# The odd mixer's modulation loads behind four input loads, and the S5 input matrix with weights and moving operand exchanged

## The chip, the core and the metric

The kernel runs on one core of a Trainium2 chip. The metric is the device time of one execution in microseconds (us): before, the median of three runs is 1391.2 us, the runs lie between 1390.48 and 1392.53. The engines named below are TensorE (PE in the rows: matmuls and transposes), VectorE (DVE), ScalarE (ACT), GpSimd (POOL) and SyncE (SP), whose queue issues most of the DMA transfers.

## The reference: what is computed

One step of a two-layer hybrid recurrent decoder for a prompt of 512 tokens and 8 single-token samples, model width 1024. Each layer has a mixer and a SwiGLU FFN, both with shift, scale and gate rows ("modulation") from a conditioning vector, and a layer norm behind each. Layer 0 mixes with gated linear attention beside an RG-LRU, layer 1 with an S5 state space model beside HGRN2. Cut to what matters here:

```python
mod = jnp.einsum('bd,de->be', cond, w_ada[l]) + b_ada[l]
sh_m, sc_m, gt_m, sh_f, sc_f, gt_f = [m[:, None, :] for m in jnp.split(mod, 6, axis=-1)]
h = x * (1.0 + sc_m) + sh_m
...
z = jnp.einsum('bld,de->ble', h, w_in).astype(jnp.float32)
u, q, f, i, g = split_cols(z, ODD_SPLITS)
y, s_re_new, s_im_new = s5_ssm(u, s_re, s_im, lam_re, lam_im, log_dt, b_re, b_im, c_re, c_im, d_skip)
...
x = layer_norm(ALPHA * x + (1.0 + gt_m) * out, ln_g[l, 0], ln_b[l, 0])
h = x * (1.0 + sc_f) + sh_f
x = layer_norm(ALPHA * x + (1.0 + gt_f) * swiglu(h, ffn_w_in[l], ffn_w_out[l]), ln_g[l, 1], ln_b[l, 1])
```

`s5_ssm` is a complex-diagonal recurrence over 32 groups of 16 channels and 64 states. The kernel runs it by chunks of eight tokens, with matrices worked out from the S5 parameters alone: the matrix from one chunk's inputs to the state, from the state to its outputs, and from inputs to outputs within a chunk.

## The kernel before

**Columns and halves.** Activations lie with channels on the partitions and 520 columns: two halves of 260, each 256 prompt tokens and four samples. A weight matrix product is done in three passes on values that are split into a high and a low part (`mm3`, lines 237 to 241, and `mmh`, lines 816 to 818, which takes one half at a time): weights 128x128, 260 columns moving.

**The weight stream.** All large weights come in one order, the list `plan` (from line 266). Each entry is one load of up to 1 MB on SyncE's queue (line 176) into one of three raw buffers. An "in", "fin" or "fout" entry is then split by ScalarE (`whi`, line 199) and VectorE (`wlo`, line 110) into one of three slots. An "ada" entry is a piece of the modulation weights: its eight matmuls (line 323, 32 weight columns each, in four column strips of TensorE) run straight from the raw buffer, and four such entries make one chunk of 1024 modulation columns, which ScalarE copies (`adasb`), TensorE transposes twice (line 147) and VectorE adds to its bias (`mod`). `mix(main, ada, first, per)` spreads the ada entries among the main ones: `first` main entries come ahead, then ada entries, `per` at a time. Line 287 does that for the odd mixer's ten input loads (`OD_COLS`: first columns 0, 256, 1024, 1280, 512, ...) and eight ada entries (`OA`: the gate of the mixer and the shift of the FFN of layer 1).

**What sets the order.** The kernel is recorded once, and a scheduler then sets the order of the instructions on every engine from its own model of their times; so an edit in one place can move others on all engines.

**The S5 preparation.** `s5_prep` works out the S5 matrices during the first half of layer 0's FFN, between that FFN's matmuls. For each of four chunks of eight groups: VectorE makes `BA` (three operations of 128x1024, with the temporary `W`), TensorE transposes it eight times (for `BATd`), and then eight matmuls (line 1620) multiply `BA` as weights (128x128 per group) with `CS` as the moving operand (16 columns per group) into `pM`, from which ScalarE copies 128x128 into `Mall` (line 1622). VectorE goes on with `CA` and `W`. `BA`, `W`, `CA` and `sb` share four buffers. `Mall` is read behind all four chunks. In the same stretch VectorE serves the FFN: `sg` multiplies a finished accumulator by its gate and so frees it, `al` is the low part of the product that the FFN's output projection (`ah`, `al`) reads.

**The passage to the odd mixer.** Layer 0's FFN ends in a layer norm, done half by half. `odd_mixer` begins with `first_units`: five units of 128 output columns (four of u, one of f), half 0 first, while the layer norm of half 1 still runs. For u the accumulator is emptied by ScalarE (`ut`, line 1671) and VectorE (`u_s`, line 1673), and for each 128 channels `Ud` is written to DRAM (line 1675), then `Usd` (line 1695). Eight gathers (line 1697) and two more (lines 1698, 1699) read them back into `u8`, all on SyncE's queue, and `s5_in` (line 1716) multiplies u8 with `BATd`. Between these the remaining units of f, q, i and g run with `mm3`. The layer norm's matmuls are lines 699 to 702.

## Time and profile before

| what | value |
|---|---|
| median of three runs | 1391.2 us (1390.48 to 1392.53) |
| the profiled execution | 1391.37 us |
| its span | 1389.4 us |
| TensorE busy | 1333.4 us (96%) |
| VectorE busy | 764.9 us (55%) |
| ScalarE busy | 498.2 us (36%) |
| GpSimd busy | 191.8 us (14%) |

The rows are of one profiled execution; its span begins with the first and ends with the last instruction, and 2.0 us of its time lie around it. All starts are us from the span's start. The median is 0.17 us under the profiled execution.

### The profile page before, as it was taken

The page shows a single profiled execution, that of the slowest core. Times are in us where ns is not written, and L with a number is a line of the kernel's source. Part 1 is how long each engine was busy: PE and PEld are TensorE (multiplying, and loading weights), DVE is VectorE, ACT ScalarE, POOL GpSimd, SP SyncE. Part 2 cuts the span into 40 slices and gives each one's busy share as a digit, 9 for nine tenths or more (in the row PEclk, how much of TensorE's full clock was granted, in tenths as well). Part 3 has the DMA queues.
Part 4 walks back from the last instruction along what each step waited for, and adds up shares of the span by engine and source line. Part 5 has one row for each costly group of instructions (what it writes and reads, how often), then busy time and mean ns, then how long its engine had stood idle before and what let it go on. Part 6 is the DMA issues. An engine that isn't in the chain of part 4 may idle for free. (4 is left out here: it accounts for less than half of the span.)

```text
span 1389.4 us, 29467 instructions
## 1 busy us (share of the span) xinstructions
PE 1333.4 (96%) x12687; PEld 1267.0 (91%) x12687; DVE 764.9 (55%) x1726; ACT 498.2 (36%) x802; POOL 191.8 (14%) x215
## 2 busy tenths in 40 slices
PE   6998999989999999999998999999999999999996
PEld 4797988989998999999988999889899999999996
DVE  4677755687997233233592785566833233232365
ACT  3555536353232222222264123363533222222231
POOL 2200010340011200000170421013500000000013
PEclk9999999999999999999999999999999999999998
DMA  9643363413345842444458446432333323221211
GB/s 277 197 152 101 91 212 120 154 48 120 116 166 205 234 152 92 152 133 158 150 200 169 131 147 216 126 126 92 101 113 107 118 95 122 92 92 54 84 62 63
DMA packets 157628, 185.53 MB, mean 134 GB/s; under 512 B 18188, under 2 KB 137354, under 8 KB 157242
## 3 DMA queue, kind: packets, MB, share of 16 engines
q1 hardware_dynamic: 151514, 166.43, 38.7%
q0 software_dynamic: 5744, 17.08, 3.8%
q8 instruction: 100, 1.64, 0.5%
q14 instruction: 30, 0.25, 0.1%
q10 hardware_dynamic: 240, 0.13, 0.0%
HBM read 167.11 MB, written 15.36 MB: 131 GB/s over the span
## 5 line engine op out<-in xcount | busy, mean ns | idle before, releaser
L237 PE MATMUL acc<-hhi,whi 128*128 128x260 f32 x1936 | 398.8, 287 | 3.0 <-ACT whi L199 1.3
L199 ACT CAST whi<-raw 128x1024 fp32r<-128x1024 f32 (+2 forms) x198 | 187.7, 955 | 587.1 <-PE acc L239 428.1
L239 PE MATMUL acc<-hlo,whi 128*128 128x260 f32 x1936 | 396.2, 286 | 1.2 <-DVE hlo L110 1.2
L241 PE MATMUL acc<-hhi,wlo 128*128 128x260 f32 x1936 | 395.1, 285 | 0.0
L110 DVE TENSOR_TENSOR wlo<-raw,whi 128x1024 fp32r<-128x1024 f32 (+2 forms) x198 | 220.2, 1116 | 222.3 <-ACT whi L199 220.7
L237 PEld LDWEIGHTS acc<-hhi,whi 128*128 128x128 f32 x1936 | 300.5, 190 | 16.1 <-issue 5.9
L239 PEld LDWEIGHTS acc<-hlo,whi 128*128 128x128 f32 x1936 | 300.6, 190 | 4.4 <-DVE hlo L110 1.7
L241 PEld LDWEIGHTS acc<-hhi,wlo 128*128 128x128 f32 x1936 | 300.9, 190 | 2.3 <-issue 1.7
L239 PE MATMUL acc<-al,whi 128*128 128x260 f32 x576 | 116.0, 283 | 2.3 <-DVE al L110 2.3
L237 PE MATMUL acc<-ah,whi 128*128 128x260 f32 x576 | 116.4, 284 | 1.4 <-DVE x L122 0.8
L241 PE MATMUL acc<-ah,wlo 128*128 128x260 f32 x576 | 115.7, 283 | 0.0
L110 DVE TENSOR_TENSOR sg<-acc,sg 128x520 f32<-128x520 f32 (+1 forms) x48 | 31.0, 653 | 112.6 <-PE acc L241 108.1
L237 PEld LDWEIGHTS acc<-ah,whi 128*128 128x128 f32 x576 | 88.3, 188 | 4.8 <-ACT whi L199 2.3
L239 PEld LDWEIGHTS acc<-al,whi 128*128 128x128 f32 x576 | 88.6, 188 | 2.5 <-DVE al L110 2.5
L241 PEld LDWEIGHTS acc<-ah,wlo 128*128 128x128 f32 x576 | 88.6, 188 | 0.0
L524 POOL TENSOR_TENSOR s<-x 128x520 f32<-128x520 f32 x4 | 6.9, 1720 | 568.1 <-ACT whi L199 321.6
L110 DVE TENSOR_TENSOR smp<-acc,gt 128x8 f32<-128x8 f32 (+1 forms) x72 | 11.6, 161 | 119.0 <-PE acc L241 94.5
L816 PE MATMUL acc<-hhi,whi 128*128 128x260 f32 x208 | 59.2, 287 | 3.3 <-ACT hhi L774 3.3
L818 PE MATMUL acc<-hlo,whi 128*128 128x260 f32 x208 | 58.8, 289 | 3.3 <-DVE hlo L767 1.9
L817 PE MATMUL acc<-hhi,wlo 128*128 128x260 f32 x208 | 58.3, 282 | 0.0
L122 DVE SCALAR_TENSOR_TENSOR x<-acc,gt,x 128x512 f32<-128x512 f32 (+1 forms) x72 | 44.8, 622 | 0.0
L323 PE MATMUL mx<-raw,condT 128*32 128x256 f32 x640 | 44.2, 384 | 0.0
(592 smaller groups left out, 2017.5 us busy)
## 6 DMA issues: line engine op xcount, KB each, us to landing
raw<-in_w_ada_dram SPq DMA_DIRECT2D x40, 1024.0 KB, 6.1
raw<-in_ffn_w_in_dram SPq DMA_DIRECT2D x40, 1024.0 KB, 5.2
raw<-in_ffn_w_out_dram SPq DMA_DIRECT2D x16, 1024.0 KB, 5.3
raw<-in_ev_w_in_dram SPq DMA_DIRECT2D x10, 1024.0 KB, 9.4
raw<-in_od_w_in_dram SPq DMA_DIRECT2D x10, 1024.0 KB, 5.9
raw<-in_w_ada_dram SPq DMA_DIRECT2D x16, 512.0 KB, 7.3
raw<-in_ffn_w_out_dram SPq DMA_DIRECT2D x16, 384.0 KB, 3.1
raw<-in_ev_w_out_dram SPq DMA_DIRECT2D x4, 1024.0 KB, 5.3
```

The lines of the kernel that those rows point to most:

```text
L110: V.tensor_tensor(out=out, in0=a, in1=b, op=op)
L122: V.scalar_tensor_tensor(out=out, in0=a, scalar=s, in1=b, op0=op0, op1=op1)
L199: S.copy(hi[:, :nk, :m], rj)
L237: T.matmul(acc[:, hf, :HN], wh[:, k - koff, :], ah(k)[:, hf, :], start=st, stop=False)
L239: T.matmul(acc[:, hf, :HN], wh[:, k - koff, :], al(k)[:, hf, :], start=False, stop=False)
L241: T.matmul(acc[:, hf, :HN], wl[:, k - koff, :], ah(k)[:, hf, :], start=False, stop=sp)
L323: T.matmul(p[32 * c:32 * c + 32, 0:256], condT[:, k0 + k, :], r[:, k, 256 * c:256 * c + 256], start=(k0 + k == 0), stop=(k0 + k == 7), til ...
L524: G.tensor_tensor(out=lnt["s1"], in0=x[:, 0] if m == 1 else lnt["s1"], in1=x[:, m], op=ALU.add)
L816: T.matmul(out, wh[:, k, :], ah(k)[:, hf, :], start=n == 0, stop=False)
L817: T.matmul(out, wl[:, k, :], ah(k)[:, hf, :], start=False, stop=False)
L818: T.matmul(out, wh[:, k, :], al(k)[:, hf, :], start=False, stop=n == len(ks) - 1)
```

## The change

There are two edits. The first changes one argument of `mix`: four of the odd mixer's input loads now come ahead of the first ada entry, where none did. The order of loads was, with the numbers of the columns and a1 to a8 for the ada entries, 0, a1, 256, a2, 1024, a3, 1280, a4, 512, 768, a5, 1536, a6, 1792, a7, 2048, a8, 2304, and it is 0, 256, 1024, 1280, a1, 512, a2, 768, a3, a4, 1536, a5, 1792, a6, 2048, a7, a8, 2304.

The second exchanges the operands of L1620. Two groups of `CS` (32 columns) are now the weights, and `BA` of one group (128 columns) moves. The eight products lie in four column strips of 32 partitions, in two blocks of 128 columns. Each product holds its group's result and that of its neighbour, which isn't used, and it is transposed. So ScalarE copies 128x256 to `mt`, TensorE transposes it twice, and ScalarE picks the right halves into `Mall` with two copies.

```diff
-        plan += mix(p_cols("in", od_in, OD_COLS), OA, 0, 1)
+        plan += mix(p_cols("in", od_in, OD_COLS), OA, 4, 1)
...
                     pM = mx()
                     for g in range(8):
-                        gg = 8 * ch + g
-                        T.matmul(pM[:, g * 16:(g + 1) * 16], BA[:, g].rearrange("p e h -> p (e h)"), CS[:, gg],
-                                 start=True, stop=True)
-                    S.copy(Mall[:, 128 * ch:128 * ch + 128], pM[:, 0:128])
+                        c, gg = g % 4, 8 * ch + g - g % 2
+                        T.matmul(pM[32 * c:32 * c + 32, 128 * (g // 4):128 * (g // 4) + 128],
+                                 CS[:, gg:gg + 2].rearrange("p a b -> p (a b)"), BA[:, g].rearrange("p e h -> p (e h)"),
+                                 start=g < 4, stop=True, tile_position=(0, 32 * c), skip_group_check=True)
+                    mt = tmp.tile([128, 256], F32, tag="t2k", name="mt")
+                    S.copy(mt, pM[:, 0:256])
+                    for q in range(2):
+                        transpose(pM[:, 256 + 128 * q:384 + 128 * q], mt[:, 128 * q:128 * q + 128])
+                    mv = Mall[:, 128 * ch:128 * ch + 128].rearrange("p (a b h) -> p a b h", b=2, h=16)
+                    for b in range(2):
+                        S.copy(mv[:, :, b], pM[:, 256:512].rearrange("p (a b d h) -> p a b d h", b=2, d=2, h=16)[:, :, b, b])
```

On TensorE in the first FFN, at the first chunk of the S5 preparation (L1620 and L147; the other rows are the FFN's matmuls), the order changes so:

```order
 L239 MATMUL acc<-hlo,whi 128x260 x2
-L1620 MATMUL mx<-CS,BA 128x16 x8
...
+L1620 MATMUL mx<-BA,CS 32x128 x8
...
+L237 MATMUL acc<-hhi,whi 128x260 x2
+L239 MATMUL acc<-hlo,whi 128x260
+L147 MATMUL mx<-ident,mt 128x128 x2
+L239 MATMUL acc<-hlo,whi 128x260
 L241 MATMUL acc<-hhi,wlo 128x260 x2
```

The eight small matmuls keep their place; the two transposes stand some 23 large matmuls behind them. In the next two chunks it is 26 and 23.

On VectorE, where the first half of that FFN ends, with the S5 preparation's last two chunks (`mod_87` and `gt` are modulation, `sg` and `al` the FFN's, `wlo` a weight split), the order was:

```order
L110 TENSOR_TENSOR CA<-XC,CT_4223 128x1024
L110 TENSOR_TENSOR W<-YC,CT_4288 128x1024
L110 TENSOR_TENSOR mod_87<-mx,vA 128x2x4x9
L110 TENSOR_TENSOR CA<-CA,W 128x1024
L128 TENSOR_SCALAR gt_5429<-mod_87 128x72
L110 TENSOR_TENSOR BA<-XB,BT 128x1024
L110 TENSOR_TENSOR sg<-acc,sg 128x520
L110 TENSOR_TENSOR W<-YB,BT 128x1024
L110 TENSOR_TENSOR wlo<-raw,whi 128x1024
L110 TENSOR_TENSOR al<-sg,ah 128x520
```

and is now:

```order
L110 TENSOR_TENSOR mod_87<-mx,vA 128x2x4x9
L128 TENSOR_SCALAR gt_5449<-mod_87 128x72
L110 TENSOR_TENSOR CA<-XC,CT_4223 128x1024
L110 TENSOR_TENSOR W<-YC,CT_4288 128x1024
L110 TENSOR_TENSOR CA<-CA,W 128x1024
L110 TENSOR_TENSOR sg<-acc,sg 128x520
L110 TENSOR_TENSOR BA<-XB,BT 128x1024
L110 TENSOR_TENSOR wlo<-raw,whi 128x1024
L110 TENSOR_TENSOR W<-YB,BT 128x1024
L110 TENSOR_TENSOR al<-sg,ah 128x520
```

Here sg has moved ahead of BA, and wlo ahead of W; the same work stands ahead of al.

On SyncE's queue in the passage to the odd mixer (L176 with `w_ada` is a modulation load, with `od_w_in` an input load) it was:

```order
L1675 DMA Ud<-ut 128x512
L176 DMA raw<-in_od_w_in_dram 128x8x256
L1675 DMA Ud<-ut 128x512 x2
L176 DMA raw<-in_od_w_in_dram 128x8x256
L1675 DMA Ud<-ut 128x512
L1695 DMA Usd<-u_s 128x4x8
L176 DMA raw<-in_w_ada_dram 128x2x1024
L1697 DMA u_8349<-Ud 16x32x64 x8
L1698 DMA u_8349<-Usd 16x32x8
L1699 DMA u_8349<-Usd 16x32x8
L176 DMA raw<-in_od_w_in_dram 128x8x256
```

and is now:

```order
L1682 DMA Ud<-ut 128x512
L176 DMA raw<-in_od_w_in_dram 128x8x256
L1682 DMA Ud<-ut 128x512 x2
L176 DMA raw<-in_w_ada_dram 128x2x1024
L1682 DMA Ud<-ut 128x512
L1702 DMA Usd<-u_s 128x4x8
L1704 DMA u_8369<-Ud 16x32x64 x8
L1705 DMA u_8369<-Usd 16x32x8
L1706 DMA u_8369<-Usd 16x32x8
L176 DMA raw<-in_od_w_in_dram 128x8x256
```

A modulation load no longer stands between `Usd` and the gathers; the input load of columns 768, ahead of the last `Ud` before, now stands behind the gathers, and a modulation load has its place. On TensorE in the same passage all modulation matmuls ahead of `s5_in` (four ada entries' worth) have moved behind its start, with eleven large matmuls. On VectorE the second split of `wx` (the first units' weights) has moved from the end of the layer norm's rows to directly behind the first, and the second copy of `u_s` stands three rows earlier.

## Rows read from the trace of the kernel before

**Rows 1.** The page's part on busy time: for each engine its busy time, its share of the span and its instructions.

```profile
PE 1333.4 (96%) x12687; PEld 1267.0 (91%) x12687; DVE 764.9 (55%) x1726; ACT 498.2 (36%) x802; POOL 191.8 (14%) x215
```

**Rows 2.** TensorE's timeline in the first FFN around one chunk's eight matmuls of L1620 (start in us, duration in us, engine, line, operation and tile, weights and moving shape, records). A duration runs to the modelled end and overlaps the next row; the difference of two starts is the time on the engine.

```profile
392.05 1.85 PE L1620 MATMUL mx<-CS,BA 128*128 128x16 f32 x16
393.75 0.48 PE L241 MATMUL acc<-hhi,wlo 128*128 128x260 f32 x2
394.08 0.40 PE L237 MATMUL acc<-hhi,whi 128*128 128x260 f32 x2
```

**Rows 3.** The view of one source line, L1620: engine, records, duration in ns (least, median, most), first and last start, form.

```profile
L1620 PE MATMUL mx<-CS,BA x64: 179/263/263, 392.1 to 440.1; 128*128 128x16 f32 x64
```

**Rows 4.** TensorE's timeline around two modulation loads' matmuls (L323) in the same stage.

```profile
417.02 1.93 PE L323 MATMUL mx<-raw,condT 128*32 128x256 f32 x32
418.88 0.51 PE L237 MATMUL acc<-hhi,whi 128*128 128x260 f32 x2
```

**Rows 5.** TensorE's timeline around two transposes (L147) in the same stage.

```profile
424.19 0.42 PE L147 MATMUL mx<-ident,adasb 128*128 128x128 f32 x2
424.37 0.48 PE L241 MATMUL acc<-hhi,wlo 128*128 128x260 f32 x2
```

**Rows 6.** TensorE's timeline where the first FFN half's output projection begins; in brackets the idle time before the row and what ended it.

```profile
427.57 0.41 PE L237 MATMUL acc<-ah,whi 128*128 128x260 f32 x2
...
429.71 0.51 PE L237 MATMUL acc<-ah,whi 128*128 128x260 f32 x2 [0.52 <-DVE sg L110]
...
434.23 0.51 PE L239 MATMUL acc<-al,whi 128*128 128x260 f32 x2 [2.33 <-DVE al L110]
```

**Rows 7.** VectorE's timeline in the same stretch.

```profile
424.38 1.23 DVE L110 TENSOR_TENSOR W<-YC,CT 128x1024 f32<-128x1024 f32 x1 [2.50 <-PE mx L1620]
...
425.67 1.22 DVE L110 TENSOR_TENSOR CA<-CA,W 128x1024 f32<-128x1024 f32 x1
...
426.92 2.12 DVE L110 TENSOR_TENSOR BA<-XB,BT 128x1024 f32<-128x1024 f32 x1
428.96 0.69 DVE L110 TENSOR_TENSOR sg<-acc,sg 128x520 f32<-128x520 f32 x1
430.42 2.02 DVE L110 TENSOR_TENSOR W<-YB,BT 128x1024 f32<-128x1024 f32 x1 [0.77 <-ACT ah L336]
432.37 1.20 DVE L110 TENSOR_TENSOR wlo<-raw,whi 128x1024 fp32r<-128x1024 f32 x1
433.49 0.68 DVE L110 TENSOR_TENSOR al<-sg,ah 128x520 fp32r<-128x520 f32 x1
```

**Rows 8.** TensorE's timeline in the passage from the first layer's FFN to the odd mixer: the modulation matmuls (L323) there, the first large matmul behind the last of the layer norm's stops (L816), and the first matmul of the S5 input (L1716).

```profile
711.06 1.50 PE L323 MATMUL mx<-raw,condT 128*32 128x256 f32 x24
...
713.13 0.64 PE L323 MATMUL mx<-raw,condT 128*32 128x256 f32 x8
...
722.54 1.07 PE L323 MATMUL mx<-raw,condT 128*32 128x256 f32 x16
725.08 0.36 PE L816 MATMUL acc<-hhi,wx 128*128 128x260 f32 x1 [1.47 <-DVE u_s L1673]
...
739.60 1.05 PE L323 MATMUL mx<-raw,condT 128*32 128x256 f32 x10
...
765.98 0.52 PE L1716 MATMUL mx<-u,bt 128*64 128x72 f32 x4 [5.94 <-DMA u<-Usd]
```

**Rows 9.** SyncE's queue in the same passage: the DMA issues (start, duration of the issue, line, destination and source, count); then the time from issue to landing (least, median, most), first that of the modulation load at 744.31, then that of the eight gathers of L1697.

```profile
742.40 0.34 SPq L1675 DMA_DIRECT2D Ud<-ut  x1
...
744.31 1.34 SPq L176 DMA_DIRECT2D raw<-in_w_ada_dram  x1
751.15 7.47 SPq L1697 DMA_DIRECT2D u<-Ud  x8
758.66 1.22 SPq L1698 DMA_DIRECT2D u<-Usd  x1
...
761.35 1.20 SPq L176 DMA_DIRECT2D raw<-in_od_w_in_dram  x1
...
DMA to landing us min/median/max: 10.8/10.8/10.8
...
DMA to landing us min/median/max: 5.3/8.3/8.8
```

**Rows 10.** VectorE's timeline ahead of the release of the accumulator (the copy of u_s, L1673).

```profile
724.11 0.42 DVE L767 TENSOR_TENSOR hlo<-h32h,hhi 128x256 fp32r<-128x256 f32 x1 [0.38 <-ACT ut L1671]
724.45 0.42 DVE L110 TENSOR_TENSOR x<-x,rs 128x256 f32<-128x256 f32 x1
724.78 0.15 DVE L1673 COPY u_s<-acc 128x4 f32<-128x4 f32 x1
```

**Rows 11.** TensorE's timeline in the odd mixer, behind the S5 input, at a stop.

```profile
819.83 0.46 PE L924 MATMUL mx<-Qs,U 128*32 128x32 f32 x33 [0.73 <-DVE U L110]
```

**Rows 12.** One row of TensorE's timeline behind a stop in the first mixer, and three rows of the view by windows: from and to, length, busy time (records) of TensorE, its weight loads, VectorE, ScalarE and GpSimd, the clock granted to TensorE as a share of full speed, busy share of the DMA engines (sum over queues), GB/s.

```profile
129.64 1.57 PE L1224 MATMUL mx<-xc,wrg 128*128 128x260 f32 x3 [2.77 <-issue]
...
130.00:134.00 4.00, 4.00 (x19) 3.68 (x19) 0.86 (x2) 3.19 (x5) 0.00 (x0) 0.60 0.02 7
...
432.00:435.00 3.00, 0.77 (x6) 0.77 (x7) 3.00 (x4) 0.17 (x1) 0.00 (x0) 1.00 0.00 0
...
766.00:771.00 5.00, 5.00 (x57) 4.86 (x58) 2.81 (x10) 0.00 (x0) 1.42 (x2) 0.50 0.64 195
```

## The prediction

> **What bounds the kernel now.** The busy table comes first: TensorE is busy 1333.4 of 1389.4 us, 96%, VectorE 55%, ScalarE 36% [rows 1]. So the time is TensorE's work plus the few places where TensorE stands still, and each edit is priced by what it does to one or the other. The two edits touch two stages, so I read those next on TensorE's timeline. In the first FFN, the eight small matmuls of L1620 come four times, once per chunk of the S5 preparation, between the large matmuls; one chunk holds TensorE from 392.05 to 393.75, 1.70 us, and the pair of large matmuls behind it then takes 0.33 us where the usual is 0.24 [rows 2]. The view by line counts 64 records for these 32 matmuls, so one matmul is two passes here [rows 3]. Soon after comes a stop of 0.52 us for sg and one of 2.33 us for al, both on VectorE [rows 6]; they are VectorE's queue, which is full at that point [rows 7]. In the passage to the odd mixer, TensorE stops 1.47 us for a released accumulator and 5.94 us for the gathered u [rows 8]; the rows of the SP queue show what lies ahead of that gather [rows 9], and VectorE's what lies ahead of that accumulator [rows 10].
>
> **The swapped operands: TensorE's work.** Before, a chunk costs 1.70 us plus 0.09 us on the matmuls behind it (0.33 less 0.24), 1.79 us [rows 2]. The new form has 32 weight columns in four column strips and 128 moving columns. The nearest rows are the modulation matmuls, which have the same 32-column strips and 256 moving columns: 32 passes from 417.02 to 418.88, so 58 ns a pass [rows 4]. For 128 columns I take half, 29 ns, since a strip row is made of columns: 16 passes are 0.46 us. The upper bound is that a pass doesn't shrink with its columns: 0.93 us. A pass below the share of its columns has no row that supports it, so 0.46 us is also the lower end. Two transposes are added, 0.18 us by the pair at 424.19 [rows 5]. I add 0.09 us three times, for entering the strips, leaving them and leaving the transposes, as on the matmuls behind L1620 [rows 2]. Together 0.91 us, so a chunk saves 0.88 us (0.41 at the upper bound).
>
> **The swapped operands: VectorE's queue.** Three chunks lie ahead of the stop for al, so TensorE comes to each point there 2.6 us sooner. What is late next is al. Before, VectorE waited until 424.38 for chunk two's matmuls, then ran W, CA, BA, sg, W, wlo, al one after another [rows 7]; BA stood ahead of sg, and so the accumulator that sg frees came 0.52 us late [rows 6]. In the new order sg stands ahead of BA. W can start at about 421.5 (424.38, less 0.88 twice, less 1.15 for this chunk's shorter matmuls), W and CA end at 423.8. The accumulator for sg is done when the out projection starts, 427.57 before [rows 6], so 425.0 now; sg 0.69 makes 425.7, BA 2.04 makes 427.7, wlo 1.12 makes 428.8, W 1.95 makes 430.8, al 0.68 makes 431.5 [rows 7]. TensorE reaches that wait at 428.8 (431.9, that is 434.23 less its wait, less 2.6, less the 0.52 that goes). So it stands 2.7 us in place of 2.33 and goes on at 431.5 in place of 434.23: 2.7 us saved, of the 3.1 that the earlier work offers. The fourth chunk lies behind and adds 0.9: **3.6 us saved**, or 1.7 with the upper price of a pass (then al ends at 432.9, 1.3 sooner, and the fourth chunk gives 0.4). The four added copies on ScalarE per chunk have cover, since ScalarE is busy 36% and Mall is read only behind all four chunks.
>
> **The modulation loads: what goes from ahead of the S5 input.** Four of the eight loads leave this stretch. A load's matmuls are 16 records and took 1.07 us at 722.54 [rows 8]. Two loads ran during the layer norm (24 and 8 records), one at 722.54, and of one more 10 records at 739.60 [rows 8], the rest of it a little later. Without the first two TensorE is through its first units' matmuls 2.1 us sooner, at 720.4, and then has nothing, since the accumulator that it waits for is freed by VectorE's copy of u_s, which ran at 724.78 [rows 10]. That copy stands three rows earlier in the new queue, because the second split of wx moved from between the layer norm's rows to behind the first split. Three rows of some 0.34 us (724.11 to 724.45, 724.45 to 724.78) and the 0.38 that VectorE waited there for ScalarE [rows 10] make 1.4; if the rows merely close up and the chain ahead of them is as late as before, 0. I take 1.3, near the rows' own sum. So TensorE stands from 720.4 to 723.8, 3.4 us in place of 1.47, and goes on 1.3 us sooner. The part load at 739.60 is gone too (1.05 us by its row [rows 8], 1.0 taken), so the last Ud write is issued 2.3 us sooner than 742.40 [rows 9].
>
> **The gathers.** Before, the order on SP was Ud, Usd, a 1 MB modulation load at 744.31, and then the gathers, which begin at 751.15, when Ud has landed, 8.75 us after its issue [rows 9]. The modulation load lands at 755.1 (10.8 us), 4.0 us behind Ud [rows 9]. The first gather takes 5.3 us, so it lands at 756.5. TensorE then waits for the Usd gather, issued at 758.66, until 765.98 [rows 8, 9]. In the new order no 1 MB load lies between. What that frees is between 0 (each gather bound by its own descriptors, issues of 7.47 us for eight) and 4.0 us (all of the load's tail); I take 2.3, a little over the middle, because the gathers' issues take 0.93 us each on the mean while the load is under way, and the issue of Ud took 0.34 [rows 9]. So the S5 input starts at 765.98 less 2.3 less 2.3, 761.4. By the Trainium skill, page "DMA: Bandwidth & Descriptors", section "Queues, rings and completion order", each DMA engine consumes its descriptors in ring order, whoever issued the work behind it. That the first gather landed 1.4 us behind the load agrees, and by that rule the whole 4.0 us would come back: 1.7 us less than my sum. The load of the input columns 768, before the last Ud write until now, goes behind the gathers on SP: the load there, at 761.35 [rows 9], is 4.6 us sooner now, 756.8, and with Ud's 8.75 us it lands near 765.5, split by 768. From the S5 input's start TensorE has 54 large matmuls (0.12 us each, 6.5), a modulation load (1.07) and the S5 matmuls to do ahead of that unit, so it gets there after 769: cover of about a microsecond, which costs what it lacks if the load takes as long as the modulation load's 10.8.
>
> **The modulation loads: what comes back.** The work is not gone. Four loads, 4.3 us, and eleven large matmuls of 0.12 us (half of a 0.24 us pair), 1.3 us, now run behind the start of the S5 input: 5.6 us against the 4.6 by which it starts sooner, so 1.0 us later. A later stop of 0.73 us [rows 11] can take some of it; I give back 0.5. Net **0.5 us lost**, between 1.2 us gained and 2.8 us lost by the ends of the gather term alone.
>
> **The clock.** A stop can cost more than itself. Behind the stop of 2.77 us at 126.9 the granted clock was 0.60 for 4 us, so 1.6 us were lost; behind the 5.94 us it was 0.50 for 5 us, 2.5 us lost; behind the 2.33 us it stayed at 1.00 [rows 12]. Both lengthened stops, 2.7 and 3.4 us, lie between. I take one fall to half clock (1.2 of 2.4 GHz) of the two, at 2.0 us between these prices; none gives 0 and both give 3.2 to 5.
>
> **Sum.** 1391.4 of the profiled execution, less 3.6, plus 0.5, plus 2.0, is 1390.3. That execution is 0.17 us above the median of the three runs, so against the median the same sum is 1390.1; I say **1390.2 us**. A measurement here can tell about 0.2%, 2.8 us, from no change, so this is no change.
>
> **Rivals.** *Faster:* neither stop drops the clock, and the gathers get back between my 2.3 and the whole 4.0 us. For it: the 2.33 us stop left the clock at 1.00, and the load landed just ahead of the first gather. Against it: the 2.77 us stop. From 1390.2 less 2.0 is 1388.2, less the further 1.7 is 1386.5; 1387.3 between. *Slower:* the release of the accumulator doesn't move, because ScalarE and VectorE are full in the layer norm; TensorE then stands 4.7 us from 720.4 to 725.08, goes on at half clock for 2.5 us, and all that the earlier start was to give there is lost. That is 1.3 more for the release and a price of 2.5 there; with the stop for al dropping too (2.5 more), the sum is 1391.4 less 3.6, plus 0.5, plus 1.3, plus 5.0, 1394.6. It decides when the release comes as late as before and both stops drop the clock; with the layer norm's alone it is 1392.1. For it: VectorE's queue is nearly without a hole there. By the Trainium skill, page "TensorE: Matmul & The Clock Gate", section "HAM oscillation — how this bites in real kernels", idle time between bursts of matmuls puts the engine to half its clock again, so both of the lengthened stops are suspects; the rows agree for the 2.77 us stop and not for the 2.33 us one. *The swap saves nothing:* passes in strips run one behind another at L1620's present 106 ns (1.70 over 16), and transposes and switches come on top: 0.45 less 0.09 a chunk more, 1.4 us in all, so 1391.4 plus 1.4, 0.5 and 2.0 is 1395.3. Against it stands the row of 58 ns with twice the columns.
>
> **How the numbers follow.** Forecast 0.48 (with its own ends of 1388.4 and 1393.5), faster rival 0.30, slower rival 0.17, no saving 0.05. The bound of 2.8 us lies at 1388.4 and 1394.0: nearly all of the faster rival lies below it, 0.29; of the others nearly the two rivals' 0.22 lies above, less a part of the slower one that stays under, 0.19; 0.52 is left for no change. The range takes in the faster rival down to near its end, 1386.0, and the slower one to its sum, 1394.8.
>
> **What would show it.** Right: L1620 at about 0.5 us a chunk; a stop for al of 2.5 to 2.9 us that ends near 431.5; no modulation matmuls from the layer norm to the S5 input, and a stop of some 3.4 us that ends near 720 of the new trace (723.8 less the first stage's 3.6); the S5 input starting near 758 (761.4 less 3.6); one of these stretches at half clock. Wrong: a chunk at over 1 us, the gathers' issues still 7.5 us long with the start no earlier than the Ud write, or a stop behind the S5 input that wasn't there before, for a weight load which the modulation loads now hold up.

## The result, and the profile of the changed kernel

The changed kernel is slower: 1399.7 us median of 13 runs (1393.3 to 1403.1) against 1390.5 us of the kernel before (13 runs, 1384.5 to 1393.2), a ratio of 1.0065 with a 95% interval of 1.0049 to 1.0081, or 9 us. The forecast was 1390.2 us, the range ended at 1394.8. The profiled execution took 1399.13 us (span 1397.4), 7.8 us over that of before, so that difference is what the traces have to explain.

The busy part of the page answers to [rows 1]:

```profile
PE 1336.2 (96%) x12695; PEld 1270.8 (91%) x12695; DVE 761.4 (54%) x1726; ACT 498.9 (36%) x810; POOL 190.4 (14%) x215
```

TensorE's busy time has hardly changed, 2.8 us more in sum; matmuls at half clock count in it with their longer time. In the first FFN the new form does what was forecast. The timeline of one chunk (answers to [rows 2, 5]) and of the restart behind the wait for al (answers to [rows 6]):

```profile
392.40 0.65 PE L1620 MATMUL mx<-BA,CS 128*32 128x128 f32 x16
392.98 0.39 PE L241 MATMUL acc<-hhi,wlo 128*128 128x260 f32 x1
...
395.85 0.38 PE L147 MATMUL mx<-ident,mt 128*128 128x128 f32 x2
395.98 0.36 PE L239 MATMUL acc<-hlo,whi 128*128 128x260 f32 x1
...
431.75 0.51 PE L239 MATMUL acc<-al,whi 128*128 128x260 f32 x2 [2.81 <-DVE al L110]
```

From 392.40 to 392.98 the sixteen passes take 0.58 us where they took 1.70, the two transposes 0.13 us. The wait for al is 2.81 us (2.7 forecast) and ends at 431.75 (431.5 forecast). Behind the first half of this FFN the program is 3.3 us ahead (a stop for x ends at 671.51, before at 674.82). The loss comes later. TensorE's stops from there on (answers to [rows 8, 11]):

```profile
671.51 0.47 PE L237 MATMUL acc<-ah,whi 128*128 128x260 f32 x2 [0.85 <-DVE x L122]
...
721.74 0.56 PE L816 MATMUL acc<-hhi,wx 128*128 128x260 f32 x1 [3.83 <-DVE u_s L1680]
...
762.19 0.40 PE L1723 MATMUL mx<-u,bt 128*64 128x72 f32 x2 [5.84 <-DMA u<-Ud]
...
779.49 0.77 PE L1723 MATMUL mx<-u,bt 128*64 128x72 f32 x16 [1.30 <-DMA bt<-BATd]
...
802.74 0.45 PE L924 MATMUL mx<-Qs,U 128*32 128x32 f32 x30 [0.59 <-issue]
...
836.89 1.01 PE L924 MATMUL mx<-Qs,U 128*32 128x32 f32 x94
840.32 0.69 PE L924 MATMUL mx<-Qs,U 128*32 128x32 f32 x34 [2.42 <-issue]
...
904.23 0.38 PE L1073 MATMUL mx<-qm,s 128*128 128x1 f32 x2 [2.33 <-DVE s L122]
```

Against before, the end of the wait for the accumulator is 3.3 us ahead (721.74 and 725.08), the start of the S5 input 3.8 us (762.19 and 765.98). At 904.23 the program is behind. That stop, for the s of the second mixer part, ended at 895.68 before, where it took 0.84 us: now 8.6 us later. So 12.3 us are lost between the S5 input's start and there. In that stretch three rows are new: 1.30 us at 779.49 for `bt`, a DMA, 0.59 us at 802.74, and above all 2.42 us at 840.32, in the middle of the 128 records of L924. The last two have "issue", that is, they wait for nothing that the profile shows. The windows (columns as in [rows 12]) give the granted clock:

```profile
722.00:728.00 6.00, 6.00 (x31) 6.00 (x31) 2.53 (x8) 2.21 (x5) 4.19 (x4) 0.56 0.01 4
...
762.00:772.00 10.00, 9.81 (x145) 8.97 (x146) 7.61 (x22) 1.55 (x2) 4.35 (x6) 0.86 0.49 143
...
841.00:850.00 9.00, 9.00 (x43) 9.00 (x43) 5.14 (x13) 3.23 (x6) 0.00 (x0) 0.50 0.32 99
...
905.00:912.00 7.00, 7.00 (x36) 6.91 (x35) 5.54 (x16) 1.15 (x3) 2.25 (x3) 0.53 0.27 81
```

The clock is at half in nearly all of 722 to 728 and 905 to 912, and in all of 841 to 850. By one minus the clock times the length, 2.6, 3.3 and 4.5 us are lost, and 1.4 behind the start of the S5 input. Before, [rows 12] had one such stretch here, 2.5 us behind the S5 input's start, and there was one of 1.7 us behind the stop at 895.68. The row of that stop and the window behind it, in the kernel before:

```profile
895.68 0.38 PE L1073 MATMUL mx<-qm,s 128*128 128x1 f32 x2 [0.84 <-DVE s L122]
...
897.80:901.20 3.40, 3.27 (x17) 2.97 (x15) 3.40 (x10) 0.57 (x1) 0.75 (x1) 0.50 0.33 100
```

The changed kernel was also at half clock from 703.4 to 706.8, where the kernel before was at 1.00. The runs say the same of the clock: the fastest of the 13 (1393.3 us) had a mean clock of 0.987, the slowest (1403.1 us) one of 0.976.

SyncE's queue ahead of the S5 input (answers to [rows 9]):

```profile
741.53 0.32 SPq L1682 DMA_DIRECT2D Ud<-ut  x1
...
750.11 4.92 SPq L1704 DMA_DIRECT2D u<-Ud  x8
```

The eight gathers issue in 4.92 us where they took 7.47. From the last write of Ud to the start of the S5 input it is 20.7 us (741.53 to 762.19), before 23.6.

### The profile page after: what moved, and what is told of

Read it like the earlier page. It is cut to its first block, busy times and chain, and to the rows that moved or that the text cites. A ratio compares the mean times of both kernels' runs of the same rounds, so it can differ in the third digit from the quotient of the medians.

```text
span 1397.4 us, 29488 instructions
## 1 busy us (share of the span) xinstructions
PE 1336.2 (96%) x12695; PEld 1270.8 (91%) x12695; DVE 761.4 (54%) x1726; ACT 498.9 (36%) x810; POOL 190.4 (14%) x215
## 5 line engine op out<-in xcount | busy, mean ns | idle before, releaser
L816 PE MATMUL acc<-hhi,whi 128*128 128x260 f32 x208 | 60.1, 291 | 3.3 <-ACT hhi L774 3.3
L323 PE MATMUL mx<-raw,condT 128*32 128x256 f32 x640 | 44.2, 384 | 0.0
```

The lines of the kernel that those rows point to most:

```text
L323: T.matmul(p[32 * c:32 * c + 32, 0:256], condT[:, k0 + k, :], r[:, k, 256 * c:256 * c + 256], start=(k0 + k == 0), stop=(k0 + k == 7), til ...
L816: T.matmul(out, wh[:, k, :], ah(k)[:, hf, :], start=n == 0, stop=False)
```

## The experiments

The theory after the result: the modulation loads alone make the loss, less by the work that they move than by longer stops of TensorE, one of them for its own code, and by the half clock behind them; the exchanged operands gain what the first FFN shows. All ratios are to the kernel before in the same session.

**One edit at a time.**

```diff
p1_loads_only:  L287 as changed, L1616 to L1629 as before
p2_swap_only:   L1616 to L1629 as changed, and
-        plan += mix(p_cols("in", od_in, OD_COLS), OA, 4, 1)
+        plan += mix(p_cols("in", od_in, OD_COLS), OA, 0, 1)
```

> Only the first edit (modulation loads behind four input loads); L1620 as before. The theory after the result: the first edit alone makes the loss, by longer stops of TensorE in the odd mixer and the half clock behind them, so this is 10 to 15 us slower than before (1401 to 1405 us), with over 25 us of half clock between 700 and 920 us. The rival, that the two edits only hurt together (the shift of the whole program by the faster first FFN moves the later stops): this is within 5 us of before.

Measured: 1403.6 us, ratio 1.0094 (1.0074 to 1.0114), 13 us slower. The theory held, also in the clock: its trace is at half clock for 30.7 us between 700 and 920. Behind 700 us it has two stops for "issue":

```profile
823.61 0.28 PE L241 MATMUL acc<-hhi,wlo 128*128 128x260 f32 x1 [1.43 <-issue]
...
842.86 1.08 PE L924 MATMUL mx<-Qs,U 128*32 128x32 f32 x102
846.35 0.51 PE L924 MATMUL mx<-Qs,U 128*32 128x32 f32 x26 [2.41 <-issue]
```

> Only the second edit (exchanged operands of L1620); modulation loads as before. The theory: the 3.5 us that the first FFN gained in the trace of the changed kernel reach the end, 1385 to 1388 us, ratio to before about 0.9975, with two half-clock spells behind 700 us as before. The rival, that the gain is given back later in the odd mixer by stops that move: within 0.1% of before.

Measured: 1388.7 us, ratio 0.9985 (0.9970 to 1.0001). By the medians 2.0 of the 3.5 us reached the end. The interval takes in both the theory's 0.9975 and the rival's 0.1%, so this run doesn't decide between them. The kernel ran once more in a later session:

> The kernel with the exchanged operands alone once more, for a closer interval. If the 3.5 us that its first FFN gains reach the end, the ratio to before is about 0.9975 again; if a part is lost behind the longer stop for al (half clock there), 0.998 to 0.999.

Measured: 1388.2 us, ratio 0.9981 (0.9969 to 0.9993), so 2.5 us faster by the medians, and now the interval leaves out no change, though not a gain of just 0.1%. In the first trace of this kernel the clock fell behind the wait for al, in the second it did not, though the wait is the same:

First trace, TensorE's timeline:

```profile
432.14 0.80 PE L239 MATMUL acc<-al,whi 128*128 128x260 f32 x2 [2.83 <-DVE al L110]
```

The window behind it:

```profile
432.20:437.00 4.80, 4.80 (x28) 4.80 (x29) 3.85 (x4) 1.46 (x2) 0.00 (x0) 0.67 0.14 25
```

Second trace, TensorE's timeline:

```profile
430.11 0.38 PE L239 MATMUL acc<-al,whi 128*128 128x260 f32 x1 [2.83 <-DVE al L110]
```

The window behind it:

```profile
430.00:435.00 5.00, 4.89 (x52) 4.61 (x52) 4.02 (x5) 2.27 (x4) 0.00 (x0) 1.00 0.20 33
```

**The stop ahead of the third accumulator, and the code.** The kernels here add matmuls with unused results in that stop, ordered behind the matmul before it and ahead of the one after it, and leave the order on TensorE otherwise as in the changed kernel.

```diff
+                    if fillers and hf == 0 and i == 4:
+                        pf = mx()
+                        for n in range(fillers):
+                            m_ = T.matmul(pf[:, :HN], wsl[0][0][:, n % 8, :], hhi[:, n % 8, 0, :], ...)
fill_wait: fillers 24;  pad_code: fillers 64, of 32 by 32, 32 columns;  pad_whole_block: 128 of these
```

> The changed kernel with 24 additional large matmuls (2.9 us of work whose result is not read) on TensorE in the 3.8 us stop ahead of the third accumulator of the odd mixer's first units; the order on all engines is otherwise the changed kernel's. If the half clock behind that stop costs what its rows show (722 to 728 at 0.56, 2.6 us), the S5 input starts 2 to 3 us sooner, and the time falls by 2 to 3 us against the changed kernel. It also moves all later code of TensorE by 48 instructions. If the stop costs only its own length and the wait for the gathers takes up what lies ahead of it, the S5 input starts at the same time.

> The changed kernel with 64 tiny matmuls (32 by 32, 32 columns, result not read) in the same stop as in the kernel with the filling: the order is otherwise the changed kernel's, but all later code of TensorE lies 128 instructions further on. The theory that the stop of 2.42 us at 840.3 (which waits for nothing that the profile shows) waits for TensorE's code, 16 KB or 256 instructions at a time: the stop goes or moves to another place, and with it the half clock from 840 to 850; about 5 us faster than the changed kernel if no other such stop arises. The rival, that the stop belongs to its instruction: it stays at the same matmul.

Measured: filled 1392.1 us, ratio 1.0016 (1.0000 to 1.0032); with 64 tiny ones 1394.5 us, ratio 1.0023 (1.0006 to 1.0040). Both are faster than the changed kernel (1.0049 to 1.0081), and neither has the stop at L924 any more. In the first the clock also stays full behind the accumulator:

Windows of the filled kernel:

```profile
722.00:728.00 6.00, 4.74 (x39) 4.56 (x39) 4.39 (x14) 4.31 (x10) 5.03 (x5) 1.00 0.00 1
...
841.00:850.00 9.00, 8.09 (x185) 7.68 (x184) 6.90 (x19) 5.05 (x10) 1.49 (x2) 1.00 0.59 168
```

Its TensorE timeline, at the accumulator and at the S5 input:

```profile
723.84 0.36 PE L816 MATMUL acc<-hhi,wx 128*128 128x260 f32 x1 [1.26 <-DVE u_s L1690]
...
763.54 0.47 PE L1733 MATMUL mx<-u,bt 128*64 128x72 f32 x3 [7.56 <-DMA u<-Ud]
```

For the filled kernel more came than expected (7.6 us by the medians against 2 to 3): the 48 instructions moved the code too, and with the stop at L924 its half clock is gone. The S5 input did not start sooner: it lay at 763.54, and the wait for the gathers was 7.56 us in place of 5.84; counted from a stop for hhi at the layer norm's start (703.87 in this trace, 702.16 in the changed kernel's) it came 0.4 us sooner. So the last sentence of the expectation holds: what lies ahead of that wait is taken up by it. Of the loss of some 9 us, the stop at L924 with what it brings is the larger part: the kernel with 64, whose clock still falls behind the accumulator (0.72 from 722 to 728), is 5.2 us faster by the medians. That the filling alone gained anything is not shown, since the two intervals overlap.

The tiny matmuls could have removed the stop by keeping TensorE busy, not by moving its code. The next kernel moves the code by a whole block of 256 instructions:

> The changed kernel with 128 tiny matmuls (result not read) in the stop ahead of the third accumulator, where the kernel with 64 had no stop of 2.4 us behind 836 us. 128 matmuls are 256 instructions, so TensorE's code behind them lies at the same places of its 16 KB blocks as in the changed kernel. The theory that the stop waits for a block of code: it is back at the same matmul, within one instruction, with half clock behind it, 5 us slower than the kernel with 64. The rival, that any additional matmuls that keep TensorE busy in the first stop also remove the later one: no stop of over 1 us at that place.

Measured: 1399.2 us, ratio 1.0055 (1.0034 to 1.0076), 4.7 us over the kernel with 64 by the medians (4.4 by the ratios), and as slow as the changed kernel. The stop is back at the same matmul, 1.89 us. The half clock that was expected behind it is not in the trace:

```profile
841.00:850.00 9.00, 8.65 (x104) 8.40 (x103) 5.15 (x13) 4.11 (x7) 0.00 (x0) 1.00 0.43 136
```

The traced execution took 1396.1 us, 3.1 under the median, so others may have had it. How the 4.7 us divide between the stop and the half clock behind it is not shown. The changed kernel's second trace has the stop too:

> The changed kernel once more, for a second trace. The theory: the stop of some 2.4 us for code stands at the same matmul again, with half clock behind it for some 10 us, and the stops ahead of it are within 0.5 us of the first trace's.

Measured (one execution): 1402.0 us, with the stop at 844.39 and half clock behind it for 10.2 us. The stops ahead of it were not all within 0.5 us: the wait for the gathers was 8.35 us in place of 5.84. TensorE's timelines around L924 (L934 in the padded kernels) in that place, first with 64 tiny matmuls, then with 128, then the changed kernel's second trace:

```profile
836.11 1.30 PE L934 MATMUL mx<-Qs,U 128*32 128x32 f32 x128
837.34 0.44 PE L1849 MATMUL mx<-u,kt 128*128 128x73 f32 x2
```

```profile
838.45 1.01 PE L934 MATMUL mx<-Qs,U 128*32 128x32 f32 x94
841.35 0.47 PE L934 MATMUL mx<-Qs,U 128*32 128x32 f32 x34 [1.89 <-issue]
```

```profile
841.24 1.01 PE L924 MATMUL mx<-Qs,U 128*32 128x32 f32 x94
844.39 0.47 PE L924 MATMUL mx<-Qs,U 128*32 128x32 f32 x34 [2.14 <-issue]
```

The stops of both traces of the changed kernel and of the kernel with 128 leave 34 of the 128 records; with 64 there is none. That the stop is one for code is shown by this and by a count of TensorE's instructions as recorded (matmuls, weight loads, and the some 200 of its sequencer, most of which wait for semaphores): in the 14 traces of this case there are 37 stops for "issue" of at least 0.5 us behind the first 100 us, and behind all 37 the first instruction, a matmul or its weight load, has a number that leaves 193 when divided by 256. The one at 129.64 of the kernel before ([rows 12]) is among them. Those behind 700 us:

```
kernel            stop (us)  ends at  instruction  mod 256
changed           0.59       802.74   14785        193
changed           2.42       840.32   16321        193
p1_loads_only     1.43       823.61   15297        193
p1_loads_only     2.41       846.35   16321        193
hold_load         0.99       827.82   16065        193
pad_whole_block   1.89       841.35   16577        193
changed_again     2.14       844.39   16321        193
p2_again          0.71       823.61   16065        193
two_loads_first   0.62       829.94   16065        193
pad_early         1.42       826.09   15809        193
pad_early         1.65       844.77   16577        193
```

The DMA queue for instructions moves 16,384 bytes at a time: 100 such packets for the changed kernel's 25,592 recorded instructions, 101 with 128 added matmuls, so one packet holds 256. Behind each of the 37 stops TensorE goes on 2.2 to 2.7 us after a packet started. In the changed kernel that packet starts at 837.79 and TensorE goes on at 840.32; in the kernel before one starts at 834.33 for the block that TensorE enters at 837.93, without a stop.

The block begins in the same stretch of L924 in both kernels, 81 of its 128 records in before and 94 now. What differs is the time ahead. Before, TensorE was in the preceding block for 6.4 us (0.8 of it a wait), and the packet started 2.8 us behind its entry; now the preceding block has fewer large matmuls and more of L924's small ones, TensorE is through with it in 4.7 us, and the packet started 4.6 us behind its entry. Why it starts so late is not shown by an experiment. Two loads are under way there, the second modulation load of the first row below (issued at 831.24) and the input load of the second, and the DMA engines move 351 GB/s from 833 to 838. But before the change two loads were under way too, with 358 GB/s from 831.54 to 834.33, so the loads alone don't tell it. SyncE's issues in the changed kernel:

```profile
822.14 9.47 SPq L176 DMA_DIRECT2D raw<-in_w_ada_dram  x2
834.32 0.37 SPq L176 DMA_DIRECT2D raw<-in_od_w_in_dram  x1
```

The last kernel asks whether the placing can be used: the exchanged operands alone, with all code from the first mixer on moved by 128 instructions.

```diff
                 for k in lag[f]:
+                    if k == 6:
+                        pf = mx()
+                        for n in range(64):  # ordered behind the matmul before, ahead of the next
+                            m_ = T.matmul(pf[0:32, 0:32], hhi[:, 0, 0, 0:32], hhi[:, 0, 0, 0:32], ...)
```

> The exchanged operands alone, with 64 tiny matmuls (results not read) ahead of the first mixer, near 50 us, so that all later code of TensorE lies 128 instructions further on; the order of the first mixer also shifts somewhat on TensorE, VectorE and ScalarE. The stop of some 3 us for code at 129 us, which all kernels here have, goes or shortens if the boundary of the block there comes where less data moves: then 2 to 4 us faster than the exchanged operands alone, 1384 to 1386 us. If the stretch of tiny matmuls from 115 to 130 us is longer than the blocks can be brought in, a stop of that size only moves, and the time is the same.

Measured: 1396.6 us, ratio 1.0043 (1.0023 to 1.0062), 8 us over the exchanged operands alone. The stop at 129 stayed, and others came or grew:

```profile
114.41 0.42 PE L933 MATMUL mx<-X 64*32 64x32 f32 x15 [1.83 <-issue]
...
128.71 0.53 PE L933 MATMUL mx<-X 64*32 64x32 f32 x22 [3.25 <-issue]
...
826.09 0.28 PE L239 MATMUL acc<-hlo,whi 128*128 128x260 f32 x1 [1.42 <-issue]
...
844.77 0.34 PE L1849 MATMUL mx<-X,ct 128*128 128x73 f32 x2 [1.65 <-issue]
```

With 0.89 at 117.86 that is 9.0 us of stops for code, where the traces of the exchanged operands alone have 4.3 (1.03, 3.31) and 3.2 (1.45, 1.07, 0.71). The order of the first mixer differs too, so not all of the 8 us is shown to be the code's; but the placing was for the worse, and both sentences of the expectation missed.

**The gathers.** The load that stood ahead of the gathers is held until behind them, in the kernel with the exchanged operands alone.

```diff
+                    if plan[self.dma] == OA[4]:
+                        tc.add_manual_dep(d.ins, last["gather"].ins.name, NOSYNC, reason="behind the gathers")
```

> The kernel with the exchanged operands alone (modulation loads as before), with the one modulation load that stood between the write of Usd and the gathers held until behind the gathers on SyncE's queue. If the gathers are slowed by that load, their eight issues take under 5.5 us in place of 7.5 and the S5 input starts 2 to 4 us sooner than with the exchanged operands alone, and as that load's work was done only at some 795 us, most of it reaches the end: 1385 to 1387 us. If the gathers go by their own descriptors, the same time within 1 us.

Measured: 1390.4 us, ratio 1.0002 (0.9987 to 1.0016): no gain. SyncE's issues and, under them, TensorE's row at the start of the S5 input, of both kernels:

The exchanged operands alone:

```profile
740.75 0.36 SPq L1682 DMA_DIRECT2D Ud<-ut  x1
...
742.67 0.38 SPq L176 DMA_DIRECT2D raw<-in_w_ada_dram  x1
749.39 6.86 SPq L1704 DMA_DIRECT2D u<-Ud  x8
```

```profile
763.26 0.40 PE L1723 MATMUL mx<-u,bt 128*64 128x72 f32 x2 [4.86 <-DMA u<-Usd]
```

With the load held:

```profile
738.35 0.36 SPq L1684 DMA_DIRECT2D Ud<-ut  x1
...
747.19 5.40 SPq L1706 DMA_DIRECT2D u<-Ud  x8
...
755.37 1.23 SPq L176 DMA_DIRECT2D raw<-in_w_ada_dram  x1
```

```profile
760.73 0.47 PE L1725 MATMUL mx<-u,bt 128*64 128x72 f32 x3 [6.91 <-DMA u<-Usd]
```

The issues shorten from 6.86 to 5.40 us, as far as expected (though the filled kernel, which has no load there either, takes 6.56), but from the write of Ud to the start of the S5 input it is 22.5 us (740.75 to 763.26) and 22.4 us (738.35 to 760.73). The theory that the load costs the gathers 2 to 4 us fell. Nor did the changed kernel gain there: that stretch is 20.7 us in its first trace and 23.2 in its second (743.77 to 766.93), and 21.7 in the second of the exchanged operands alone (737.22 to 758.96), so it varies by 2 to 3 us whatever stands ahead.

> The kernel with the exchanged operands alone, with 36 additional large matmuls (4.3 us, results not read) on TensorE in the 4.9 us wait for the gathers, released by the first gather. If the half clock behind that wait is a cost of its own, the granted clock stays at 1.00 there and the time falls by 1.5 to 3.4 us against the exchanged operands alone; the S5 matmuls behind it also stand a little differently. If filling only moves the half clock to a later place or delays the S5 input, the same or slower.

```diff
+                    if p0 == 0:
+                        prev = T.matmul(pf[0:32, 448:512], ident[0:16, 0:32], u8[0:16, 0, 8:72], start=True, stop=True)
+                        for k in range(36):  # each ordered behind the one before, ahead of the S5 matmuls
+                            m_ = T.matmul(pf[:, 0:HN], hhi[:, k % 8, 0, 0:128], hhi[:, k % 8, 0, :], ...)
```

Measured: 1391.1 us, ratio 1.0019 (1.0000 to 1.0039): slower than the exchanged operands alone. In TensorE's order the filling came ahead of some 5 us of large matmuls that without it run before the wait, and the clock fell all the same behind the shorter stop ahead of it (0.79 from 749 to 757). So this run doesn't tell what the half clock costs there.

TensorE's timeline:

```profile
751.56 0.27 PE L1723 MATMUL mx<-u,ident 16*32 16x64 f32 x2 [1.91 <-DMA u<-Ud]
751.76 6.11 PE L1725 MATMUL mx<-hhi 128*128 128x260 f32 x36
...
759.61 1.24 PE L1731 MATMUL mx<-u,bt 128*64 128x72 f32 x32 [0.42 <-DMA u<-Usd]
```

The window around the first of them:

```profile
749.00:757.00 8.00, 6.09 (x39) 5.82 (x38) 0.00 (x0) 0.79 (x2) 0.00 (x0) 0.79 1.47 107
```

**Other versions.**

> The exchanged operands alone, with 20 additional large matmuls (2.4 us, results not read) in TensorE's stop for al in the first FFN. If the half clock behind that stop, which the trace of the exchanged operands alone shows (0.67 over 4.8 us), is a cost of its own, 1 to 2 us faster than the exchanged operands alone, with no half clock between 425 and 440 us. If the clock at that place is not what the time goes by, the same.

In this kernel the added matmuls write beside the accumulator in its own bank, and that changes part of the first FFN's sums. Measured: 1387.3 us, ratio 0.9978 (0.9965 to 0.9990), against 0.9981 of the exchanged operands alone in the same session: no difference that can be told. In its trace the stop for al is 0.65 us and the clock stays at 1.00 from 425 to 440, so the 1 to 2 us that were to come from the clock there did not reach the end. The same trace has half clock for 10 us from 834.5, behind a stop of 1.82 us for another reason (`vt`, from ScalarE): a stretch as long as the changed kernel's can follow a stop that is not one for code.

> Both edits, but with two input loads ahead of the first modulation load in place of four, so that one more modulation load falls into the layer norm. The theory: with less work taken from the stop ahead of the third accumulator it is 1 to 3 us shorter and less work comes behind the S5 input, so the time lies between the exchanged operands alone (1388 to 1390 us) and the changed kernel (1399.7 us), at some 1391 to 1395 us, and higher if TensorE's code meets a stop of 2 us at a new place.

```diff
+        plan += mix(p_cols("in", od_in, OD_COLS), OA, 2, 1)
```

Measured: 1390.7 us, ratio 0.9991 (0.9973 to 1.0009), slightly under what was expected. The accumulator's wait is 2.40 us, between 1.43 and 3.83, and behind 700 us no stop for code is over 0.7 us. By the medians the exchanged operands alone remain the fastest version whose sums are the reference's; its interval and this one overlap.

## Why the prediction was wrong

**What held.** The operands: 0.58 us a chunk plus 0.13 for the transposes, against 0.46 and 0.18; the wait for al 2.81 us against 2.7; 3.3 us ahead behind it against 3.6. Of the two lengthened stops one dropped the clock, as forecast: behind the accumulator's 2.6 us were lost (2.0 forecast), behind al's none in the first trace. (The row behind al's stop in [rows 12] lies mostly within the stop, but from 434.2 to 439 the clock was at 1.00 too.)

**The step that failed** is the sum of what goes from ahead of the S5 input and what comes back behind it. The prediction paid for 5.6 us of returning work with a start that is 4.6 us sooner and 0.5 that a later stop takes. Counted from the stop for x, the start came 0.5 us sooner in the first trace and 2.1 later in the second, and the stops behind took nothing: in the first trace they grew by 2.7 us, and the half clock there by 3.4.

**The release of the accumulator** was to come 1.3 us sooner. From the end of the stop for x to the end of the wait for the accumulator it is 50.2 us (671.51 to 721.74) where it was 50.3 (674.82 to 725.08): it did not move. That the stop's 3.83 us lie near the 3.4 forecast is luck, since this term had failed. It is what the slower rival said of the release; with al's stop at full clock that rival's own sum is 1392.1 us, so it too lacks what came behind the S5 input.

**The term of the clock was mis-sized.** "I take one fall to half clock of the two, at 2.0 us" counted two places. There were others: 10 us of half clock behind the stop at L924 (4.5 us lost in the window shown) and 7 us behind the stop at 904.23 (3.3 us), both behind the S5 input, where the prediction's sum has stops only as time to give back (0.5 us). Among its signs of being wrong it did name a new stop there, for a weight load; what came was one for code and one for `bt`.

**The rival that was missing.** A stop for TensorE's code was in the rows that the prediction used: 2.77 us at 129.64 with "issue" [rows 12] was read as a sample of the clock's behaviour and not asked what it waited for. In the changed kernel TensorE reaches the end of a block within L924 before the next block is there. Removing that stop (64 tiny matmuls) gave 5.2 us back, putting it back (128) cost 4.7.

**The gathers' term was wrong.** "That frees between 0 and 4.0 us; I take 2.3": holding the load shortened the issues by 1.5 us and the stretch from Ud to the S5 input by 0.1. The lower end of that term was the right one. The rule on ring order that the prediction took from the Trainium skill (page "DMA: Bandwidth & Descriptors", section "Queues, rings and completion order") gave 4.0 us as the price of the load. The page says it of the descriptors of one ring; the load and the gathers are both on SyncE's queue, and with the load held none of the 4.0 us came, so the measurement decides against that price here. In the first trace of the changed kernel the stretch is 2.9 us shorter than before, near the 2.3, but in the second 0.4: that too is luck. In the first trace the S5 input came 3.8 us sooner where 8.2 (3.6 and 4.6) were forecast: Ud was written 0.9 us sooner and not 5.9, as the accumulator came sooner by the first stage's gain alone, and from there to the write of Ud it took 19.8 us in place of 17.3, with 2.6 lost to the half clock.

**The work that came back** was sized rightly: by the records, the 64 matmuls of the four loads and eleven large ones stand behind the S5 input's start, seven of the eleven ahead of the stop at 904.23. The kernel with 64, which has no stop for code there, agrees with the 5.6 us, being 5.8 us over the exchanged operands alone (1.0023 and 0.9981); but it has longer stops too, 2.45 us for s where they have 0.83, so it doesn't show the work alone.

**The sum of the traces.** From the S5 input's start to the end of the stop at 904.23: 5.1 us of moved work (4.3 and seven large matmuls); stops of 1.30, 0.59, 2.42 and 2.33 us where there were 0.73, 0.79, 1.62 and 0.84, 2.7 more; lost clock of 5.9 us (1.4 and 4.5) where it was 2.5. That makes 11.2 of the 12.3 us. Behind it the half clock takes 3.3 us where before some 1.7 were lost, but that doesn't show at the end: to the end of the span it is 493.1 us where it was 493.7. So by stages the changed kernel gains 3.3, 0.5 and 0.6 us and loses 12.3, which makes the 8.0 between the spans.

## What to carry to other kernels

Work that fills a stop of the busiest engine may be worth more than its length: here taking it away lengthened the stop, lowered the clock behind it and moved the work to where it was added to the time. Any edit that changes the number or order of TensorE's instructions moves its code against blocks of 256 and changes how long a block lasts; where small matmuls bring a block to its end before the next one is there, that was worth some 5 us here. Look at stops for "issue" in the trace, and test a suspect with a padding of half a block and of a whole one. A gain in one stage is booked only when the stages behind it have been read for new stops.

## What was not expected of the hardware

- TensorE's stops for "issue": 37 of 37 at an instruction number of 193 modulo 256, 0.59 to 3.39 us each, and each over 2.2 to 2.7 us after the start of a packet of 16,384 bytes of code. The stop near 129 us stands in all 14 traces (1.07 to 3.39 us).
- The clock is not the same for the same stop: behind 2.83 us it fell to half in one trace (0.67 over 4.8 us) and stayed at 1.00 in another. Of the eleven traces with a wait of 2.8 to 3.2 us for al, six have half clock behind it. Between runs of the changed kernel the mean clock went from 0.976 to 0.987 and the time from 1403.1 to 1393.3 us.
- The same gathers, behind the same queue, took from 20.7 to 23.2 us from the write of Ud to the S5 input in two traces of one kernel; one trace is not enough to price them.
